# A feed-forward down projection by seven products instead of eight, with its weight sums kept in DRAM

## The chip, the cores and the metric

The kernel runs on one core of one Trainium2 chip. The metric is the device time of one execution in microseconds (us). Before the change it is 3280.02 us, the median of three runs (3275.47, 3280.02 and 3282.64). The engines are TensorE (PE in the profile; PEld is its loading of weights), VectorE (DVE), ScalarE (ACT), GpSimd (POOL) and SyncE (SP). In this kernel SP issues every data transfer. SBUF is the on-chip memory of 128 partitions, PSUM the eight banks into which TensorE writes, DRAM the memory off the core.

## The reference

One layer of a streaming encoder is computed for 2048 prompt frames and 32 sample frames, 2080 columns of 1024 features in all. The layer is token mixing, then attention to 256 memory tokens, then a SwiGLU feed-forward sub-layer; each is wrapped in RMSNorm before and after, and added to the residual. The change touches only the feed-forward part:

```python
def swiglu(h, w_gate, w_up, w_down):
    return (jax.nn.silu(h @ w_gate) * (h @ w_up)) @ w_down

xp = xp + rmsnorm(swiglu(rmsnorm(xp, g_pre_ffn), w_ffn_gate, w_ffn_up, w_ffn_down), g_post_ffn)
```

`w_gate` and `w_up` are 1024 x 2816, `w_down` is 2816 x 1024, all float32.

## The kernel before, in words

**Precision.** A float32 operand is split into a high part (a ScalarE cast) and a low part (a subtraction, on VectorE for weights and for the input, on POOL for the gated activations); this is `split` (lines 424 and 425). `mm3` (line 485) makes a product of three matmuls: high by high, high by low, low by high.

**Blocks and groups.** In the feed-forward stage (line 1710 on) the columns are cut into three blocks `CF` of two halves each, 2 x 348, 2 x 346 and 2 x 346 columns; `ci` numbers the half. The hidden width of 2816 is 22 tiles of 128 rows, and two tiles make a group, 11 groups in all.

**Gate and up by seven products.** `gate_up(g)` (line 1808) makes one group of hidden rows for both column halves. The weight block (1024 x 256) and the input block (1024 x 2n) are each cut in two by two, and the 2 x 2 product is made from seven products instead of eight, of sums of the quarters (`seven_mov` for the input, once in a block, into seven tiles mf; `seven_sta` for the weights, for each group; `unit`, line 1782, for the products, in the PSUM banks X, Y and Z). A unit is 7 x 12 matmuls, a group two units. SiLU and the product with the up part follow, and POOL and ScalarE split the result into the tiles u.

**Down by eight.** `down` (line 1844) takes one group (in the last block the last two together). For each column half and each of eight output tiles it makes one PSUM tile pdn from the group's two row tiles, six matmuls, and VectorE copies it into the accumulator acc (first group, line 571) or adds it (line 532). With the last group come the squares of the post-norm sum (`square`). The weights (`down_w`) are fetched raw, 512 KB a row tile, and split again in each block.

**Buffers.** A block has two accumulators, taken from a pool of two (`xp`), so a new block's accumulator waits for the release of an old one. Raw weights have four buffers of 512 KB (`WRB`), split weights eight (`WSB`), u three, the raw input four (`stage`). The products have six PSUM banks.

**Ends of blocks.** `finish` (line 1872) of a block normalises each half, adds the residual fetched from DRAM and stores it; it is issued after the next block's first and second gate-and-up group. In the last block, half 1 is finished by `finish` and half 0 transposed by `finish_rows`.

**Order.** `Order` (from line 48) writes the order of every engine's instructions and of SP's transfers: it plays the whole program through with a cost for each instruction and the buffer counts, some passes forward and back, and fixes the best order that it found. Each queue then runs strictly in that order.

Of the kernel before, what the change touches and what calls it, by code (L numbers as in the profile page):

```python
# [18 lines left out]
P = 128  # L19
D = 1024  # L20
# [373 lines left out]
def encoder_step(ctx, tc, ins, outs):  # L394
# [118 lines left out]
    qmd = [dpool.tile([D, n], F32, name=f"qmd{b}") for b, (_, n) in enumerate(CB)]  # L513
    biasd = dpool.tile([HA, 768], F32, name="biasd")
# [1196 lines left out]
    UB, WRB, WSB, SGB = 3, 4, 8, 5  # L1711
    with ExitStack() as ph:
# [21 lines left out]
        def ffn_raw(b):  # L1734

            s, n = CF[b]
            raw = {}
            for kh, c in ((0, 0), (0, 1), (1, 1), (1, 0)):
                r = stage(f"hr{b}_{kh}{c}")
                for bb, lo, hi, off in pieces(CB, s + c * n, s + c * n + n):  # L1740
                    SP.dma_start(r[:, :, off : off + hi - lo], h2d[bb][kh * 512 : kh * 512 + 512, lo:hi].rearrange("(k p) n -> p k n", p=P))
                raw[kh, c] = r[:, :, :n]
            return raw

        def ffn_ops(b, raw):

            n = CF[b][1]
            ops = []

            def put(src, eng):  # L1750
                m_ = mps[len(ops)].tile([P, 2, HK, 348], F32R, tag="mov", name=f"mf{b}_{len(ops)}")
                split(m_[:, 0, :, :n], m_[:, 1, :, :n], src, eng)
                ops.append((m_[:, 0, :, :n], m_[:, 1, :, :n]))

            seven_mov(raw, put)
            return ops
# [19 lines left out]
        def prod(ps, w, m, first, last):  # L1776
            mm3(ps, [((w[0][:, k], w[1][:, k]), (m[0][:, k], m[1][:, k])) for k in range(HK)], first, last, not first)
# [23 lines left out]
        QS = ((0, 1), (1, 1), (0, 0), (1, 0))  # L1801
        with tc.high_priority(offset=PRI):
            ops = ffn_ops(0, ffn_raw(0))
        late = []
        for b, (s, n) in enumerate(CF):
            ssqs, silu = {}, []
            acc = [xp.tile([P, KT, 348], F32, tag="acc", name=f"acc{b}_{ci}") for ci in range(2)]
            def gate_up(g, own=False):
                sg = {q: small(sp, "sg", f"sg{b}_{g}_{q[0]}{q[1]}", SGB)[:, :n] for q in QS}
# [218 lines left out]
```

## Time and profile before

| what | value |
|---|---|
| median of three runs | 3280.02 us |
| profiled execution, first to last instruction (its own time is known only by this span) | 3277.0 us |
| TensorE busy | 3156.6 us (96%) |
| VectorE busy | 2416.9 us (74%) |
| ScalarE / POOL busy | 1719.9 / 717.1 us |
| mean granted TensorE clock | 0.984 |
| matmuls of the down projection (tile pdn) | 3168, from 1884.5 to 3261.9 us |
| mean DMA rate | 148 GB/s |

A row of the profile's groups gives line, engine, operation, the tile written and the tiles read, shapes and count, then busy time and mean length, then the idle time of the engine just before these instructions and what ended it. Matmuls are pipelined, so their recorded lengths overlap. A row of waits reads: engine, tile and line, what it waited for, us in total, times, longest.

### The profile page before, as it was taken

The numbers are of one execution on the slowest core, as the hardware profiler recorded it, in microseconds if no ns is written. First come the engines' busy times: TensorE is split into PE (matmuls) and PEld (weight loads), VectorE is DVE, ScalarE is ACT, GpSimd is POOL, SyncE is SP. The second block draws the span as 40 slices with busy tenths as digits, with TensorE's granted clock in tenths as the row PEclk, the third lists the DMA queues.
The fourth block names the chain that finished last, engine by engine and source line by source line (L and its number), as shares of the span: only waits on it lengthen the run. The fifth ranks groups of instructions, "written<-read, shape, count | busy, mean of one in ns | idle before, by whom it ended". The sixth has DMA issues, their size and how long they took to land.

```text
span 3277.0 us, 57899 instructions
## 1 busy us (share of the span) xinstructions
PE 3156.6 (96%) x21387; PEld 3022.0 (92%) x21387; DVE 2416.9 (74%) x4474; ACT 1719.9 (52%) x3706; POOL 717.1 (22%) x933
## 2 busy tenths in 40 slices
PE   7898999799999999999999899999899999899998
PEld 7888999698888888999999799999899999899998
DVE  7976976576575756777777877777977778977776
ACT  5645655656676666566665643334544334444344
POOL 0200100345474545410101111111211111311111
PEclk9999999899999999999999999999999999999999
DMA  5569273876585757765655522222432222422223
GB/s 150 178 168 297 101 222 120 262 227 193 177 269 152 239 169 229 221 191 179 204 175 179 166 91 71 76 78 78 136 111 78 76 73 63 130 79 77 78 78 96
DMA packets 490076, 486.31 MB, mean 148 GB/s; under 512 B 78528, under 2 KB 427881, under 8 KB 489793
## 3 DMA queue, kind: packets, MB, share of 16 engines
q1 hardware_dynamic: 489793, 482.61, 47.2%
q8 instruction: 168, 2.75, 0.3%
q14 instruction: 115, 0.94, 0.1%
HBM read 369.78 MB, written 113.83 MB: 148 GB/s over the span
## 4 chain that ended last, share of the span: by engine, by line
PE 88%; DVE 5%; DMA 3%; ACT 2%; issue 1%; SPq 1%; POOL 0%; DVEq 0%; ACTq 0%; POOLq 0%
PE pdn L485 15%; PE pg_X L485 8%; PE pu_X L485 7%; PE wops L1329 6%; PE mops L485 5%; PE mqps L485 4%; PE pg_Y L485 4%; PE pu_Y L485 4%; PE po L1063 4%; PE s L1058 2%; PE pg_Z L485 2%; PE pu_Z L485 2%; PE pt L1083 2%; PE ms L485 2%; PE g_s L1263 2%; PE wva_X L485 1%
## 5 line engine op out<-in xcount | busy, mean ns | idle before, releaser
L485 PE MATMUL pdn<-u,wd 128*128 128x346 f32 (+1 forms) x3168 | 520.2, 323 | 25.7 <-DVE acc L571 24.4
L485 PEld LDWEIGHTS pdn<-u,wd 128*128 128x128 f32 x3168 | 509.4, 190 | 27.7 <-DVE acc L571 25.3
L425 POOL TENSOR_TENSOR u<-sg,u 128x346 fp32r<-128x346 f32 (+1 forms) x132 | 165.4, 1264 | 1152.9 <-ACT u L424 611.7
L424 ACT CAST wg_s<-wg_r 128x512 fp32r<-128x512 f32 x231 | 139.1, 620 | 480.5 <-PE pdn L485 183.5
L532 DVE TENSOR_TENSOR acc<-acc,pdn 128x346 f32<-128x346 f32 (+1 forms) x464 | 235.8, 513 | 89.1 <-PE pdn L485 88.8
L485 PE MATMUL pg_X<-mf,wg_s 128*128 128x346 f32 (+1 forms) x1584 | 278.1, 324 | 6.6 <-ACT wg_s L424 5.3
L485 PE MATMUL pu_X<-mf,wu_s 128*128 128x346 f32 (+1 forms) x1584 | 275.2, 322 | 0.0
L485 PEld LDWEIGHTS pg_X<-mf,wg_s 128*128 128x128 f32 x1584 | 258.4, 190 | 8.2 <-ACT wg_s L424 5.7
L485 PEld LDWEIGHTS pu_X<-mf,wu_s 128*128 128x128 f32 x1584 | 256.9, 189 | 0.4
L1329 PE MATMUL wops<-om,wo_s 128*128 128x512 f32 (+1 forms) x960 | 214.4, 362 | 0.5 <-POOL om L430 0.5
L485 PE MATMUL mops<-mo,wmo_s 128*128 128x416 f32 x960 | 193.7, 353 | 2.1 <-DVE y L1671 1.2
L425 DVE TENSOR_TENSOR wu_s<-wu_r,wu_s 128x512 fp32r<-128x512 f32 x231 | 155.0, 696 | 39.1 <-ACT wu_s L424 39.0
L425 DVE TENSOR_TENSOR wd<-wd_r,wd 128x512 fp32r<-128x512 f32 x132 | 93.8, 715 | 121.7 <-ACT wd L424 121.6
L485 PEld LDWEIGHTS mops<-mo,wmo_s 128*128 128x128 f32 x960 | 177.1, 188 | 6.7 <-issue 1.9
L1329 PEld LDWEIGHTS wops<-om,wo_s 128*128 128x128 f32 x960 | 149.3, 188 | 20.5 <-issue 2.2
L485 PE MATMUL mqps<-m,wmq_s 128*128 128x416 f32 x768 | 163.6, 357 | 4.7 <-DVE m L430 4.2
L424 ACT CAST wu_s<-wu_r 128x512 fp32r<-128x512 f32 x231 | 136.6, 619 | 50.0 <-DVE wu_r L529 23.2
L425 DVE TENSOR_TENSOR wg_s<-wg_r,wg_s 128x512 fp32r<-128x512 f32 x231 | 158.7, 694 | 0.9 <-ACT wg_s L424 0.7
L1063 PE MATMUL po<-prt,v 128*128 128x128 f32 x1120 | 158.1, 281 | 1.2 <-PE mkps L1329 0.9
L1063 PEld LDWEIGHTS po<-prt,v 128*128 128x128 f32 x1120 | 145.3, 194 | 9.3 <-issue 2.9
L485 PE MATMUL pu_Y<-mf,wu_s 128*128 128x346 f32 (+1 forms) x792 | 140.1, 324 | 7.4 <-DVE up L532 5.7
L485 PEld LDWEIGHTS mqps<-m,wmq_s 128*128 128x128 f32 x768 | 139.8, 189 | 6.8 <-DVE m L430 4.4
(450 smaller groups left out, 7197.0 us busy)
## 6 DMA issues: line engine op xcount, KB each, us to landing
wg_r<-in_w_ffn_gate_dram SPq DMA_DIRECT2D x66, 512.0 KB, 4.4
wu_r<-in_w_ffn_up_dram SPq DMA_DIRECT2D x66, 512.0 KB, 3.5
wd_r<-in_w_ffn_down_dram SPq DMA_DIRECT2D x66, 512.0 KB, 3.4
wmq_r<-in_w_mq_dram SPq DMA_DIRECT2D x80, 256.0 KB, 3.0
wmo_r<-in_w_mo_dram SPq DMA_DIRECT2D x80, 256.0 KB, 3.0
q<-qd SPq DMA_DIRECT2D x32, 512.0 KB, 4.5
wo_r<-in_w_o_dram SPq DMA_DIRECT2D x64, 256.0 KB, 4.1
nb<-nbd SPq DMA_DIRECT2D x16, 640.0 KB, 7.6
```

What stands on the lines that cost most here:

```text
L424: ACT.copy(hi, src)
L425: (lo_eng or DVE).tensor_tensor(out=lo, in0=src, in1=hi.bitcast(F32), op=ALU.subtract)
L485: PE.matmul(ps, lhsT=a, rhs=b, start=first and i == 0, stop=last and i == len(seq) - 1, skip_group_check=skip)
L532: eng.tensor_tensor(out=out, in0=a, in1=b, op=ALU.add)
L1058: PE.matmul(ps_out, lhsT=q[:, 2 * i + e, q0 : q0 + nq], rhs=ks[:, e, k0 : k0 + ncol], start=i == 0, stop=i == 1)
L1063: PE.matmul(po[:, e * P : e * P + n], lhsT=v[:kk, j, e * 64 : e * 64 + P], rhs=prt[:kk, j, :n], start=j == 0, stop=j == len(rows) - 1)
L1083: PE.transpose(ptp[:kk, j, :n], pr[:n, c0 : c0 + kk], ident[:n, :n])
L1263: PE.matmul(sps[bk, li, :], lhsT=lh, rhs=rh, start=True, stop=True)
L1329: PE.matmul(ps, lhsT=a, rhs=b, start=i == 0, stop=i == len(seq) - 1)
```

## The change

Groups 0 to 9 of a block form five pairs. For a pair, the down weights (512 rows of hidden x 1024) and the gated activations (512 rows x 2n columns) are each cut in two by two, and the pair's contribution is made from seven products of sums of quarters. A product has four PSUM tiles, each of two row tiles (six matmuls). Products 0, 2, 4 and 6 go one after the other into the same four banks X; after each of them VectorE adds the banks, as they then stand, to one quarter of the accumulators. Products 1 and 3 do the same in Y, and product 5 in Z. Group 10 keeps the old way, alone, in all three blocks.

The weight sums are made in block 0, split, used, and stored split in DRAM (`wdd`); blocks 1 and 2 fetch the split tiles from there. The activations of three groups are now kept unsplit (`gt`), summed in place and split by POOL and ScalarE in pieces of 2n columns. The two accumulators last through all blocks. The input's staging tiles have half the size (two of four feature tiles, so every block's input is fetched and split in two halves), the residual is fetched and the result stored in quarters instead of halves, and the normalisation factor stays in PSUM.

The diff, cut to its core:

```diff
+    wdd = [dpool.tile([14 * P, 1024], F32, name=f"wdd{j}") for j in range(NF // 4)]
...
-    UB, WRB, WSB, SGB = 3, 4, 8, 5
+    UB, WRB, WSB, GTB = 3, 4, 8, 3
...
+        gt = pool("cgt", GTB)
...
-        pt = ph.enter_context(tc.tile_pool(name="cpt", bufs=1, space=PSUM, **RW))
-        pn = ph.enter_context(tc.tile_pool(name="cpn", bufs=1, space=PSUM, **RW))
+        pn = ph.enter_context(tc.tile_pool(name="cpn", bufs=2, space=PSUM, **RW))
+        accs = [xp.tile([P, KT, 348], F32, tag="acc", name=f"acc{ci}") for ci in range(2)]
         def stage(name):
-            return gp.tile([P, HK, 348], F32, tag="stage", name=name)
+            return gp.tile([P, 2, 348], F32, tag="stage", name=name)
...
+            def u_split(src, name):
+                t = uu.tile([P, 2, 2, 348], F32R, tag="u", name=name)[:, :, :, :n]
+                split(t[:, 0], t[:, 1], src, POOL)
+                return t
...
+            XYZ = (0, 2, 4, 6, 1, 3, 5)
+            def down_sums(j):
+                w = {}
+                with tc.high_priority(offset=PRI):
+                    if b:
+                        for i in XYZ:
+                            w[i] = [wsp(f"wd{b}_{j}_{i}{a}") for a in range(2)]
+                            for a in range(2):
+                                SP.dma_start(w[i][a].bitcast(F32).rearrange("p e m -> p (e m)"), wdd[j][(2 * i + a) * P : (2 * i + a + 1) * P, :])
+                        return w
+                    fs = [[down_raw(4 * j + 2 * k + a) for k in range(2)] for a in range(2)]
+                    def put(i, k, h):
+                        w[i] = [wsp(f"wd{b}_{j}_{i}{a}") for a in range(2)]
+                        for a in range(2):
+                            split(w[i][a][:, 0], w[i][a][:, 1], fs[a][k][:, h])
+                            SP.dma_start(wdd[j][(2 * i + a) * P : (2 * i + a + 1) * P, :], w[i][a].bitcast(F32).rearrange("p e m -> p (e m)"))
+                    def each(f, k, h, x, y):
+                        for a in range(2):
+                            f(DVE, fs[a][k][:, h], fs[a][x[0]][:, x[1]], fs[a][y[0]][:, y[1]])
+                    put(0, 0, 0)
+                    each(sub, 0, 0, (0, 0), (0, 1))
+                    each(add, 0, 1, (0, 1), (1, 1))
+                    put(1, 0, 1)
+                    each(sub, 0, 1, (1, 1), (0, 0))
+                    put(2, 0, 1)
+                    put(4, 0, 0)
+                    put(6, 1, 1)
+                    each(sub, 0, 1, (1, 0), (0, 1))
+                    put(3, 0, 1)
+                    put(5, 1, 0)
+                return w
...
+            def down_seven(j, us):
+                w = down_sums(j)
+                u0, u1 = us
+                b11, b12, b21, b22 = u0[:, :, 0], u0[:, :, 1], u1[:, :, 0], u1[:, :, 1]
+                m = {0: u_split(b11, f"u{b}_{j}_0")}
+                sub(DVE, b12, b22, b12)
+                add(DVE, b11, b11, b12)
+                m[2] = u_split(b11, f"u{b}_{j}_2")
...
+                def prods(i, ps, first):
+                    for q in range(HK):
+                        c = slice(q * P, q * P + P)
+                        mm3(ps[q], [((w[i][a][:, 0, c], w[i][a][:, 1, c]), (m[i][:, 0, a], m[i][:, 1, a])) for a in range(2)], first, True, not first)
+                X = [bank(f"pdX{b}_{j}_{q}") for q in range(HK)]
+                for i, ci, hf in ((0, 0, 0), (2, 1, 0), (4, 1, 1), (6, 0, 1)):
+                    prods(i, X, i == 0)
+                    for q in range(HK):
+                        put_acc(ci, hf * HK + q, X[q], j == 0)
...
-                r = rstd_of(np_, psn[:, :n], n, D, f"n5_{b}_{ci}_r", 2, "nsq", 348)
+                ACT.activation(r, r, AF.Ln, bias=eps_t, scale=1.0 / D)
+                ACT.activation(r, r, AF.Exp, scale=-0.5)
...
+            for g in range(NG):
+                held.append(gate_up(g))
                 if late:
                     late.pop(0)()
+                if not last and g == NG - 2:
+                    raw = ffn_raw(b + 1, 0)
+                if not last and g == NG - 1:
+                    ops = []
+                    ffn_ops(b + 1, 0, raw, ops)
+                    ffn_ops(b + 1, 1, ffn_raw(b + 1, 1), ops)
+                if g and g % 2 == 0:
+                    down_seven(g // 2 - 1, held[g - 2 : g])
```

More of the change, by code (lines that the diff above doesn't have):

```diff
@@ L1842, in square, with put_acc, bank @@
                     add(DVE, ssqs[ci], ssqs[ci], sq)
-            def down(gs, us, cis=(1, 0), dn=None):
-                dn = dn or [down_w(2 * g + j) for g in gs for j in range(2)]
-                us = [ut for u in us for ut in u]
+            def put_acc(ci, m, ps, first):
+                a = acc[ci][:, m, :n]
+                if first:
+                    out(DVE.tensor_copy, a, ps)
+                else:
+                    out(add, DVE, a, a, ps)
+            def bank(name):
+                return pd.tile([P, 512], F32, tag="dense", name=name)[:, :n]
@@ L1855, in down @@
-                        if gs[-1] == NF // 2 - 1:
-                            square(ci, m)
-                            if last and ci == 0:
-                                ACT.mul(acc[ci][:, m, :n], acc[ci][:, m, :n], gains["g_post_ffn"][:, m : m + 1])
+                        ps = bank(f"pdn{b}_{g}_{m}_{ci}")
+                        mm3(ps, [(dn[a][m], (us[ci][:, 0, a], us[ci][:, 1, a])) for a in range(2)])
+                        put_acc(ci, m, ps, False)
+                        square(ci, m)
@@ L1859, in down @@
+                        if last and ci == 0:
+                            ACT.mul(acc[ci][:, m, :n], acc[ci][:, m, :n], gains["g_post_ffn"][:, m : m + 1])
                 return dn
```

131 lines of the change are left out of this document (68 added, 63 removed).

## The prediction

> **What bounds the kernel now.** I read the page first (shares, then the chain), then a table by stretches of the feed-forward stage, then TensorE's waits there, then the groups of instructions by shape.
>
> ```profile
> span 3277.0 us, 57899 instructions
> PE 3156.6 (96%) x21387; PEld 3022.0 (92%) x21387; DVE 2416.9 (74%) x4474; ACT 1719.9 (52%) x3706; POOL 717.1 (22%) x933
> PE 88%; DVE 5%; DMA 3%; ACT 2%; issue 1%; SPq 1%; POOL 0%; DVEq 0%; ACTq 0%; POOLq 0%
> L485 PE MATMUL pdn<-u,wd 128*128 128x346 f32 (+1 forms) x3168 | 520.2, 323 | 25.7 <-DVE acc L571 24.4
> ```
>
> The chain that ends last is TensorE for 88%, and the down projection (pdn) is one of its largest pieces: 3168 matmuls. The mean of 323 ns is of overlapping records, so the price of a matmul comes from stretches where TensorE never stops. Below are eight whole groups of block 0 and of block 1, and then the two stretches in which one block gives way to the next.
>
> ```profile
> 1908.40:2245.60 337.20, 337.20 (x2117) 337.20 (x2116) 245.51 (x422) 133.98 (x260) 43.26 (x33) 1.00 0.24 77
> 2403.20:2738.90 335.70, 335.70 (x2112) 335.70 (x2111) 246.30 (x421) 133.74 (x260) 42.59 (x32) 1.00 0.24 78
> 2300.00:2400.00 100.00, 86.62 (x528) 85.34 (x527) 90.16 (x138) 50.48 (x94) 26.14 (x24) 0.95 0.48 149
> 2800.00:2900.00 100.00, 88.21 (x533) 87.24 (x532) 86.71 (x139) 49.53 (x93) 27.99 (x26) 0.93 0.33 108
> ```
>
> The columns are stretch, length, then busy time and count of PE, PEld, DVE, ACT and POOL, then clock, DMA share and GB/s. In the first two rows TensorE is busy for every microsecond: 337.20/2117 = 159.3 ns a matmul of 348 columns, 335.70/2112 = 159.0 ns of 346. VectorE does 245.51/4 = 61.4 us in each 84.3 us (two groups), 73%. The last two rows lose time: 528 and 533 matmuls of 159 ns are 84.0 and 84.7 us of 100. So a block change costs 16.0 and 15.3 us. The waits say why:
>
> ```profile
> PE pdn L485 <- DVE acc L571: 24.4, 3, 11.9
> PE pu_Y L485 <- DVE up L532: 5.7, 1, 5.7
> PE pg_X L485 <- ACT wg_s L424: 5.3, 1, 5.3
> PE pg_X L485 <- ACT pg_c L571: 0.2, 1, 0.2
> ```
>
> The first down product of a block is copied into an accumulator that the last block is still normalising and storing; TensorE stands, and the clock column shows that it runs slower after.
>
> **The change part by part.**
>
> *Fewer products.* In each block ten of the eleven groups form five pairs. A pair took 2 groups x 2 row tiles x 8 output tiles x 2 column halves x 3 = 192 matmuls and takes 7 x 4 x 2 x 3 = 168. That is 24 x 5 x 3 = 360 fewer, which is also the difference of the two programs' instruction lists; the stages ahead are the same but for a little order late in the memory attention. 120 x 159.3 + 240 x 159.0 ns = **-57.3 us**, all on the engine that sets the end.
>
> *Accumulators.* They were taken anew by each block and first written one group into it. Now they last, and the first write comes behind three groups of gate and up (3 x 168 x 159 ns = 80 us after the change of block) and waits only for the rows that it overwrites. The old block's normalisation is issued inside those 80 us. I take away the whole loss of both stretches, **-31.3 us**; at worst one store stays late (0), at best all of it goes.
>
> *VectorE, block 0.* Rows for the prices; one run of four splits gives the issue time:
>
> ```profile
> 1846.64 2.49 DVE L425 TENSOR_TENSOR wu_s<-wu_r,wu_s 128x512 fp32r<-128x512 f32 x4
> L425 DVE TENSOR_TENSOR wd<-wd_r,wd 128x512 fp32r<-128x512 f32 x132 | 93.8, 715 | 121.7 <-ACT wd L424 121.6
> L532 DVE TENSOR_TENSOR acc<-acc,pdn 128x346 f32<-128x346 f32 x304 | 154.7, 513 | 60.3 <-PE pdn L485 60.2
> L425 DVE TENSOR_TENSOR mf<-hr,mf 128x1384 fp32r<-128x1384 f32 x14 | 22.3, 1596 | 1.1 <-ACT mf L424 1.1
> ```
>
> Four splits in 2.49 us are 0.60 us each, some 0.09 less than their recorded length, since records overlap. By the same step an add from PSUM issues every 0.43, and half of the 1384-wide split takes about 0.79. A pair adds 6 splits of weights (14 for 8), 8 weight sums and 4 sums of the gated activations, and loses 4 adds from PSUM (28 for 32): 14 x 0.60 + 4 x 0.79 - 4 x 0.43 = +9.8 us. VectorE goes from 61.4 of 84.3 to 71.2 of 168 x 3 x 159 ns = 80.2 us, 89%. It still fits beneath TensorE, but two places are bare. (1) The eighth and later weight tiles wait for one of eight buffers: the tile pair of product 3 takes the buffers of product 1, which runs right ahead of it, so a ScalarE cast stands open. (2) All four raw buffers hold the pair's rows until the last splits, so the next gate weights are fetched late; the product that they must beat is 3.8 us away.
>
> ```profile
> L424 ACT CAST wd<-wd_r 128x512 fp32r<-128x512 f32 x132 | 81.4, 621 | 6.2 <-ACT wd L424 3.0 <-ACT sg L1813 1.0 <-PE pg_X L485 0.8
> wg_r<-in_w_ffn_gate_dram SPq DMA_DIRECT2D x66, 512.0 KB, 4.4
> wd_r<-in_w_ffn_down_dram SPq DMA_DIRECT2D x66, 512.0 KB, 3.4
> ```
>
> (1) costs a cast, 0.62, and a handover, some 1 us; (2) a 4.4 us landing and a cast against 3.8 us and a little, so 0 to 4. I take 3 us a pair, **+15** (0 to 40, the upper end from the rivals below). The 14 stores of a pair go through SP's queue, and the next group's four raw loads stand among them, the first behind the tenth tile's store, the last behind the fourteenth's; each of those tiles is split by the time that the load's raw buffer is free, so the queue adds nothing more.
>
> *VectorE, blocks 1 and 2.* No splits or sums of weights there: -8 x 0.60 + 3.2 - 1.7 = -3.3 us a pair; 58 of 80 us. This was hidden time and I price it at nothing. ScalarE (133.98/4 = 33.5 us a pair) and POOL (10.8) gain some 5 and 7 us in block 0 and stay far below.
>
> *Tiles from DRAM.* A pair loads 14 x 512 KB = 7.3 MB where it loaded 2.1. SP holds each load until its buffer is free, and the next group's raw weights stand behind the fourteenth, whose buffer is free once three of seven products are done: 15 us ahead of need, against the 4.4 us above. The queue carries more than this; the DMA view from 1760 to 1890 us, in 40 slices:
>
> ```profile
> GB/s 5 143 51 329 341 365 372 371 321 131 236 220 334 292 208 5 232 292 0 214 4 211 249 357 160 5 2 208 244 131 138 260 201 95 125 6 164 305 220 140
> ```
>
> At 365 GB/s 524 KB pass in 1.4 us; a product uses one in 12 x 159 ns = 1.9 us. I put **+3** in all for ten pairs.
>
> *Input in halves.* The staging tiles shrink to half, so the second half of a block's input is fetched only when the first has been summed. At the first change of block, 37 VectorE instructions stand behind the last down add until the last half is split: 17 half-wide of 0.79, 17 weight operations of 0.60 and 3 adds, 25 us, with some 6 us of matmuls left after it, against 26.7 us of gate and up. So 5 us, and about 3 for the slower clock, as in the stretches above. At the second change the list has the last half split ahead of the last down adds: 2. **+10** (0 to 31, today's loss). At the start of the stage the second halves are fetched behind stores of the last attention block: **+3** (-5 to +8, about the 5.3 and 5.7 waits above).
>
> *The end.*
>
> ```profile
> 3248.53 13.66 PE L485 MATMUL pdn<-u,wd 128*128 128x346 f32 x83
> 3255.01 2.73 DVE L1883 SCALAR_TENSOR_TENSOR acc<-acc,g_post_ffn,n_r 128x346 f32<-128x346 f32 x4
> 3260.96 0.48 ACT L1841 ACTIVATE sq<-acc 128x346 f32<-128x346 f32 x1
> 3261.47 0.59 ACT L1858 ACTIVATE acc<-acc,g_post_ffn 128x346 f32<-128x346 f32 x1
> 3268.20 3.03 DVE L1923 SCALAR_TENSOR_TENSOR xtl<-ytl,rl,xtl 128x512 f32<-128x512 f32 x4 [0.70 <-PE ytl L1919]
> ```
>
> The last two groups shared one down pass; its second half (13.66 us of matmuls) covered the normalisation of the first half. Now that pass has one group, 7.6 us, and the changed list puts the normalisation behind it: 8 scalings of 0.68, 4 adds and two ScalarE passes of 0.5, some 8 us, come ahead of the closing scalings; ScalarE's 8 x (0.48 + 0.59) = 8.6 us also outlast 7.6. **+9** (4 to 12).
>
> *Sum*: 3277.0 - 57.3 - 31.3 + 15 + 3 + 10 + 3 + 9 = 3228.4 for the span. The profiled execution's own time is known only by its span, which is 3.0 below the median of the runs, 3280.02; with the same 3.0 around it I forecast **3231 us**.
>
> **A rule that speaks against it.** POOL's splits get twice as wide.
>
> ```profile
> L425 DVE TENSOR_TENSOR wd<-wd_r,wd x132: 678/693/1457, 1883.9 to 3230.2; 128x512 fp32r<-128x512 f32 x132
> L425 POOL TENSOR_TENSOR u<-sg,u x132: 923/1335/1487, 1884.5 to 3231.1; 128x346 fp32r<-128x346 f32 x88, 128x348 fp32r<-128x348 f32 x44
> ```
>
> The same split of 128x512 takes from 678 to 1457 ns and the same POOL operation from 923 to 1487: each is at times held by the other. A POOL operation of double width (35 a pair in block 0's five pairs, 7 each) lasts some 1.8 to 2.5 us. If each held VectorE for its whole length less a little, 7 x 1.3 = 9 us come on top of 71.2, and VectorE, at 80, is the bound of block 0; with some loss at each handover I put 5 us more on a pair than the 3 above. That is five pairs x 5 us, and it is a rival below. The Trainium skill states it as a rule (SBUF — State Buffer, section "Who interferes with whom"): a VectorE instruction with two SBUF inputs contends with a GpSimd one that reads SBUF, and whoever comes second waits for the whole instruction. The trace agrees in that 1457 is about 678 plus a POOL operation; medians of 693 say that it is rare so far.
>
> **The rivals.** (a) *VectorE becomes the bound of block 0*, as just told: +25 beyond the forecast's +15, about **3256**. For it: 89% before any holding. Against it: the 2300 row has 90.16 us of VectorE in 100, and the wait there was for the accumulator, not for a split.
>
> (b) *Slower: the handover of an accumulating bank.* Each product is added out of PSUM before the next goes into the same four banks; TensorE returns to a bank after 18 matmuls, 2.9 us. In a pair six products wait so. If an add comes late by t, the cost is 15 x 6 x t = 90 t; from t = 0.55 us it eats the whole gain, at 1 us it gives 3231 + 90 = **3321**. For it: VectorE's queue is in order and the adds stand among splits and sums. Against: gate and up do the same at 12 matmuls, 1.9 us, and the wait row shows 0.2 us in all for it.
>
> (c) *Slower: loads do not overlap.* At one 3.4 us landing after another 14 loads take 48 us and have 13 + 25; 9.5 us x 10 pairs give **3326**. The GB/s row speaks against it.
>
> **How the numbers follow.** Forecast 0.60, range of its own 3200 to 3250 (its bounds do not fall together); (a) 0.20; (b) 0.10; (c) 0.04; the rest, small stalls that together eat about the gain, 0.06: 0.02 faster, 0.03 within 0.2% (6.6 us, about what a measurement of this kernel can tell from no change), 0.01 slower. Faster 0.60 + 0.20 + 0.02 = 0.82, same 0.03, slower 0.10 + 0.04 + 0.01 = 0.15. The range 3195 to 3276 holds the forecast's terms and (a) and leaves out (b) and (c).
>
> **What would show it.** Right: 360 fewer matmuls, no TensorE wait for the accumulator copies, VectorE near 90% in block 0 and 75% after, pair periods of 83 and 80 us. Wrong: TensorE waiting for adds from pdX or pdY (b), for weight splits over 3 us a pair (a), or for DMA landings in blocks 1 and 2 (c), or a half clock in the granted-clock slices of block 0, where short stalls would be paid twice.

## The result, and the profile after

The changed kernel takes 3239.64 us (median of four runs, 3234.99 to 3241.13) where the kernel before took 3279.58 beside it: a ratio of 0.9876, 95% interval 0.9862 to 0.9890. The forecast was 3231. The profiled run took 3241.13 us, 1.8 more than its span.

The lines of the page that answer those of before: the span, the engines, the chain that ended last, and the new loads.

```profile
span 3239.3 us, 57597 instructions
PE 3110.5 (96%) x21027; PEld 2969.1 (92%) x21027; DVE 2448.5 (76%) x4513; ACT 1709.8 (53%) x3656; POOL 751.6 (23%) x912
PE 86%; DVE 5%; DMA 3%; issue 2%; ACT 2%; SPq 1%; POOL 1%; DVEq 0%; POOLq 0%; ACTq 0%
wd<-wdd SPq DMA_DIRECT2D x140, 512.0 KB, 4.8
```

There are 360 matmuls fewer, and TensorE still carries the chain. Where the time went is seen in stretches of the feed-forward stage that both kernels share: each block's opening (its first three groups and the down products among them), six further groups, and its end (the last two groups). The columns are those of the prediction's table. First the kernel before, then the changed kernel, each with block 0's opening, its six groups, its end, the opening of block 1, the end of block 1 and the opening of block 2.

```profile
1820.80:1950.60 129.80, 119.83 (x700) 115.84 (x701) 108.54 (x178) 64.65 (x116) 17.54 (x15) 0.95 0.40 127
1950.60:2203.10 252.50, 252.50 (x1587) 252.50 (x1586) 182.87 (x312) 99.95 (x193) 32.45 (x24) 1.00 0.24 76
2203.10:2302.50 99.40, 99.40 (x626) 99.40 (x626) 78.47 (x126) 43.63 (x77) 12.23 (x10) 1.00 0.22 70
2302.50:2430.20 127.70, 114.32 (x702) 113.04 (x702) 111.82 (x176) 61.72 (x116) 28.33 (x26) 0.96 0.44 137
2682.20:2781.40 99.20, 99.20 (x626) 99.20 (x625) 78.70 (x128) 43.90 (x78) 12.60 (x10) 1.00 0.22 71
2781.40:2908.40 127.00, 115.21 (x702) 114.24 (x701) 110.27 (x174) 61.22 (x116) 28.89 (x26) 0.95 0.36 116
```

```profile
1822.60:1956.50 133.90, 117.09 (x677) 113.03 (x677) 122.16 (x192) 67.80 (x119) 21.39 (x13) 0.90 0.53 168
1956.50:2200.10 243.60, 242.68 (x1515) 240.73 (x1514) 213.23 (x353) 110.23 (x206) 38.12 (x21) 1.00 0.47 162
2200.10:2302.70 102.60, 99.17 (x601) 97.02 (x600) 90.43 (x150) 46.83 (x85) 16.65 (x9) 0.98 0.48 168
2302.70:2430.40 127.70, 115.09 (x678) 112.41 (x677) 110.83 (x179) 62.28 (x112) 32.64 (x24) 0.93 0.54 175
2430.40:2671.50 241.10, 241.10 (x1514) 241.10 (x1513) 174.56 (x289) 89.43 (x165) 36.79 (x21) 1.00 0.44 145
2671.50:2768.30 96.80, 95.96 (x603) 95.68 (x602) 86.20 (x137) 44.76 (x78) 14.92 (x8) 1.00 0.48 153
2768.30:2879.20 110.90, 108.97 (x678) 107.67 (x678) 95.27 (x162) 56.68 (x102) 33.00 (x24) 1.00 0.51 169
```

The loss of a stretch is its length less its matmuls at 159.2 ns: 127.70 - 678 x 0.1592 = 19.8 us in the opening of block 1. The first change of block (end of block 0 and opening of block 1) lost -0.3 + 15.9 = 15.6 us before and loses 6.9 + 19.8 = 26.7 now, 11.1 more. The second lost 14.7 and loses 0.8 + 3.0 = 3.8, 10.9 less. The two cancel. The same loss for every kernel that was run, in us, with its time ("before" and "after" mean the two kernels, and what follows the comma is the edit made to it):

| kernel | opening 0 | six groups of 0 | end of 0 | opening 1 | end of 1 | opening 2 | time | ratio to before |
|---|---|---|---|---|---|---|---|---|
| before | 18.4 | -0.2 | -0.3 | 15.9 | -0.5 | 15.2 | 3279.6 | |
| after | 26.1 | 2.4 | 6.9 | 19.8 | 0.8 | 3.0 | 3239.6 | 0.9876 |
| before, lasting accumulators | 18.4 | -0.2 | -0.3 | 12.1 | -0.3 | 13.2 | 3276.7 | 0.9980 |
| before, halves | 19.3 | 0.1 | -0.3 | 13.8 | -0.5 | 14.2 | 3275.8 | 0.9982 |
| before, both | 19.3 | 0.1 | -0.3 | 10.9 | -0.5 | 9.3 | 3269.7 | 0.9966 |
| after, sums in each block | 26.3 | 2.2 | 6.5 | 24.9 | 5.7 | 24.7 | 3283.9 | 1.0010 |
| after, light last pair | 26.0 | 2.0 | 1.7 | 12.0 | 1.0 | 3.0 | 3224.3 | 0.9825 |
| after, additions on VectorE | 25.8 | 2.9 | 6.7 | 20.2 | 1.0 | 7.6 | 3244.0 | 0.9888 |
| after, normalisation first | 25.8 | 2.0 | 7.0 | 12.1 | 1.0 | 3.4 | 3232.0 | 0.9855 |
| after, copies on ScalarE | 21.1 | 1.1 | 6.8 | 17.5 | 0.8 | 2.4 | 3230.0 | 0.9843 |
| after, low parts on VectorE | 23.9 | 1.7 | 14.4 | 5.2 | -0.3 | 3.7 | 3228.8 | 0.9841 |
| after, product moved at the end | 25.8 | 1.8 | 7.0 | 18.3 | 1.0 | 2.9 | 3237.4 | 0.9868 |
| after, three edits | 20.6 | 1.1 | 6.2 | 11.0 | 0.8 | 3.1 | 3226.7 | 0.9836 |
| after, four edits | 20.8 | 0.3 | 11.7 | 5.3 | 0.9 | 3.1 | 3220.5 | 0.9815 |

How far do these figures repeat? The kernel with the product moved at the end has the changed kernel's order of instructions in the feed-forward stage up to 3189 us, so its row is the same work once more: the opening of block 1 differs by 1.5 us, the six groups by 0.6, the other stretches by 0.3 or less. Differences of that size are not told from the spread of a stretch.

TensorE's waits of the changed kernel from 2240 to 2440 us, around the first change (what it waited for, us in total, times, longest):

```profile
PE pdX L485 <- issue: 7.3, 1, 7.3
PE pg_Z L485 <- ACT wg_s L424: 3.9, 1, 3.9
```

The 7.3 us have no releaser by the profile. VectorE's rows at their end show it, in order of time (start, us, operation):

```profile
2396.63 1.54 DVE L1980 SCALAR_TENSOR_TENSOR acc<-acc,g_post_ffn,n_ps 128x348 f32<-128x348 f32 x3
...
2402.13 1.98 DVE L1823 TENSOR_TENSOR g<-g,up 128x346 f32<-128x346 f32 x1
2404.03 0.93 DVE L572 COPY acc<-pdX 128x346 f32<-128x346 f32 x2
```

TensorE goes on at 2404.64, just behind the first copy out of PSUM into the accumulator (2404.03). That copy stood in VectorE's queue behind the old block's normalisation (the scalings of L1980) and behind sums and products of gate and up, one of which took 1.98 us. The stretch of the stall and the one behind it:

```profile
2397.00:2405.00 8.00, 0.72 (x4) 0.47 (x3) 7.91 (x12) 0.77 (x1) 8.00 (x7) 0.72 1.05 395
2405.00:2411.00 6.00, 6.00 (x23) 6.00 (x23) 3.13 (x5) 0.00 (x0) 0.77 (x1) 0.52 1.05 378
```

During the stall VectorE is busy for 7.91 of 8.00 us, and GpSimd for all of them. And the stall is paid again in clock: right behind it the granted clock is 0.52 and a matmul takes 6.00/23 = 0.26 us, 23 x 0.1 = 2.3 us more.

The 3.9 us wait is for the cast of a gate weight of block 1's first group. VectorE was behind there too: ScalarE had cast the first of these weights at 2285.33 us, as soon as it had landed, and VectorE took up its low part at 2296.64, 11 us later, behind splits of the next block's input and additions of pdn.

```profile
2285.33 0.62 ACT L424 CAST wg_s<-wg_r 128x512 fp32r<-128x512 f32 x1 [0.21 <-DMA wg_r<-in_w_ffn_gate_dram]
2296.64 0.69 DVE L425 TENSOR_TENSOR wg_s<-wg_r,wg_s 128x512 fp32r<-128x512 f32 x1
```

### The profile page after: what moved, and what is told of

Its sections match the earlier page's. It is cut to its first block, busy times and chain, and to the rows that moved or that the text cites. A ratio compares the mean times of both kernels' runs of the same rounds, so it can differ in the third digit from the quotient of the medians.

```text
span 3239.3 us, 57597 instructions
## 1 busy us (share of the span) xinstructions
PE 3110.5 (96%) x21027; PEld 2969.1 (92%) x21027; DVE 2448.5 (76%) x4513; ACT 1709.8 (53%) x3656; POOL 751.6 (23%) x912
## 4 chain that ended last, share of the span: by engine, by line
PE 86%; DVE 5%; DMA 3%; issue 2%; ACT 2%; SPq 1%; POOL 1%; DVEq 0%; POOLq 0%; ACTq 0%
PE pg_X L485 7%; PE pu_X L485 7%; PE pdX L485 7%; PE wops L1330 6%; PE mops L485 6%; PE mqps L485 4%; PE po L1064 4%; PE pg_Y L485 4%; PE pu_Y L485 4%; PE pdY L485 3%; PE s L1059 2%; PE pt L1084 2%; PE pg_Z L485 2%; PE pu_Z L485 2%; PE g_s L1264 2%
## 5 line engine op out<-in xcount | busy, mean ns | idle before, releaser
L425 POOL TENSOR_TENSOR u<-g,u 128x692 fp32r<-128x692 f32 (+1 forms) x111 | 199.0, 1799 | 1043.3 <-ACT u L424 862.6
L485 PE MATMUL pdX<-u,wd 128*128 128x346 f32 (+1 forms) x1440 | 241.2, 326 | 10.3 <-issue 7.3
L485 PEld LDWEIGHTS pdX<-u,wd 128*128 128x128 f32 x1440 | 234.8, 192 | 12.6 <-issue 8.3
L424 ACT CAST u<-g 128x692 fp32r<-128x692 f32 (+1 forms) x111 | 84.2, 773 | 231.2 <-PE pdX L485 171.7
L425 DVE TENSOR_TENSOR wu_s<-wu_r,wu_s 128x512 fp32r<-128x512 f32 x231 | 166.9, 746 | 27.3 <-ACT wu_s L424 27.1
L485 PE MATMUL pg_Y<-mf,wg_s 128*128 128x346 f32 (+1 forms) x792 | 141.1, 326 | 1.7 <-ACT wg_s L424 1.4
L533 DVE TENSOR_TENSOR acc<-acc,pdX 128x346 f32<-128x346 f32 (+1 forms) x192 | 96.4, 513 | 59.1 <-PE pdX L485 58.6
```

Source lines behind the costliest of these rows:

```text
L424: ACT.copy(hi, src)
L425: (lo_eng or DVE).tensor_tensor(out=lo, in0=src, in1=hi.bitcast(F32), op=ALU.subtract)
L485: PE.matmul(ps, lhsT=a, rhs=b, start=first and i == 0, stop=last and i == len(seq) - 1, skip_group_check=skip)
L533: eng.tensor_tensor(out=out, in0=a, in1=b, op=ALU.add)
```

## The experiments

**The accumulators and the halves, each alone and together, on the kernel before.**

```diff
+        accs = [xp.tile([P, KT, 348], F32, tag="acc", name=f"acc{ci}") for ci in range(2)]
...
-            acc = [xp.tile([P, KT, 348], F32, tag="acc", name=f"acc{b}_{ci}") for ci in range(2)]
+            acc = accs
```

> The kernel before, with one edit: the two accumulators are allocated once, ahead of the loop over blocks, instead of anew in each block. The prediction's step (the losses of 16.0 and 15.3 us at the two block changes are the wait for accumulators taken anew) as it stands gives about -31 us, 3279.6 to 3248. Theory now: in this kernel the second half's normalisation is issued right ahead of the first down product of a block, so lasting accumulators alone let the copy pass only as far as rows are free, and the first wait moves to a later row; of the 11.9 us wait I expect 3 to 10 us back at each change, 3260 to 3274 in all. Rival: nothing at all (3279), because the normalisation itself is what is late.

```diff
-            return gp.tile([P, HK, 348], F32, tag="stage", name=name)
+            return gp.tile([P, 2, 348], F32, tag="stage", name=name)
...
-                    if g == NF // 2 - 3:
-                        raw = ffn_raw(b + 1)
-                    if g == NF // 2 - 1:
-                        ops = ffn_ops(b + 1, raw)
+                    if g == NF // 2 - 2:
+                        raw = ffn_raw(b + 1, 0)
+                    if g == NF // 2 - 1:
+                        ops = []
+                        ffn_ops(b + 1, 0, raw, ops)
+                        ffn_ops(b + 1, 1, ffn_raw(b + 1, 1), ops)
```

> The kernel before, with one edit: staging tiles of half the size, the input of a block fetched, summed and split in two halves, and the normalisation's residual in quarters. The prediction charged +3 at the start of the stage and +10 at the two block changes: 3293. Theory now: the halves cost this or more at the first change, since VectorE gets the second half's splits only when the first half is summed and the next weights stand behind them: 3290 to 3300. Rival: they cost nothing, the losses at the changes are those of the accumulators: 3280 +- 3.

> The kernel before, with both edits: lasting accumulators and halves, but every down product as before and no weight sums. It stands for the prediction's terms -31.3 + 10 + 3 = -18, so 3261. What the changed kernel's trace shows for the same three places (about -2, -11 and +2) would be about 3268. If it comes out at 3275 or above, the late first write (behind three groups instead of two) is what brings the gain of the second change, not the lasting accumulators.

Measured: 3276.7 (ratio 0.9980, 0.9971 to 0.9990), 3275.8 (0.9982, 0.9973 to 0.9991) and 3269.7 (0.9966, 0.9954 to 0.9977). The opening of block 1 with lasting accumulators, and two of TensorE's waits there, the longest and the one for the accumulator's copy:

```profile
2304.50:2428.40 123.90, 115.77 (x702) 114.63 (x702) 110.47 (x176) 61.20 (x116) 28.51 (x26) 0.96 0.45 142
```

```profile
PE pdn L485 <- DVE sg L1819: 6.8, 1, 6.8
PE pdn L485 <- DVE acc L571: 1.4, 1, 1.4
```

They save 3.8 us there and 2.0 in the opening of block 2, less than the 6 to 20 that I expected and a fifth of the prediction's 31.3: the 11.9 us wait for the copy becomes 1.4, and 6.8 come up in its stead, for a product of gate and up (L1819) that stands in VectorE's queue. The halves were to cost 13 or more; the openings of blocks 1 and 2 lose 2.1 and 1.0 us *less* with them, and the opening of block 0 0.9 more. So my theory of the halves fell, and 3275.8 lies a little under the rival's 3277 to 3283 as well. Together they save 5.0 and 5.9, and 3269.7 is nearest to the 3268 that was read off the changed kernel's trace. I read the wait at a block change as a full VectorE queue in which the accumulator's copy came last; the 6.8 us that came up say so. These runs keep the first write one group into the block. What the late first write alone would do on this kernel was not run.

**The weight sums in each block, on the changed kernel.** The branch that loads them is never taken, and the stores are made in block 0 alone.

```diff
-                    if b:
+                    if False:
                         for i in XYZ:
...
+                            if not b:
```

> The changed kernel, with one edit: blocks 1 and 2 compute and split the sums of the down weights again instead of loading them from DRAM (block 0 still stores them). The prediction priced the relief of VectorE in blocks 1 and 2 at nothing, and block 0's loaded VectorE at 3 us a pair; measured in block 0 are 1.0 us in a regular pair and 5.7 in the first one. Theory now: blocks 1 and 2 then look like block 0 (10 us each), and the second block change like the first (some 15 us more than now): 3240 to 3265 +- 8. Rival: only the pair price, +10 to +20, with the change of block as it is: 3250 to 3260. Second rival: VectorE at 89% is fully hidden, 3240 +- 4, and the DRAM copies are worth nothing.

Measured: 3283.9, ratio 1.0010 (1.0000 to 1.0021): the whole gain is gone. Three pairs of block 1, its end, and the opening of block 2:

```profile
2439.80:2682.20 242.40, 242.31 (x1513) 240.38 (x1512) 218.02 (x351) 110.97 (x207) 38.80 (x21) 1.00 0.24 77
2682.20:2783.60 101.40, 98.12 (x601) 96.72 (x601) 94.21 (x153) 48.13 (x89) 16.41 (x9) 0.98 0.25 78
2783.60:2916.40 132.80, 118.32 (x679) 115.16 (x678) 116.09 (x192) 67.18 (x121) 29.58 (x23) 0.92 0.38 117
```

A regular pair hardly cares: 242.4/3 = 80.8 us with VectorE busy for 218.02/242.40 = 90%, against 241.1/3 = 80.4 at 72%. The second change cares: 5.7 + 24.7 = 30.4 us lost against 3.8. TensorE's two longest waits there are for VectorE:

```profile
PE pu_X L485 <- DVE up L533: 5.3, 1, 5.3
PE pdX L485 <- DVE acc L572: 2.9, 1, 2.9
```

What DRAM buys is this 26.6 us and 5.1 at the opening of block 1. The rest of the difference of the two spans is 5 us ahead of the stage (its first matmul is at 1827.4 instead of 1822.6; the planner orders the early stages otherwise in this kernel, from 177 us on, so this part is not the edit's own work) and some us in the last pairs and the end. All three of my cases were too low: the theory ended at 3273, with 15 us more at the second change and 10 in a block; it had the place right and the size too small.

**Is it the last loaded pair of block 0?** This run leaves out the fifth pair's own weight sums: in every block that pair takes those of the fourth from DRAM. VectorE then forms and splits none for it in block 0.

```diff
-                    if b:
+                    if b or j == 4:
...
-                                SP.dma_start(w[i][a].bitcast(F32).rearrange("p e m -> p (e m)"), wdd[j][(2 * i + a) * P : (2 * i + a + 1) * P, :])
+                                SP.dma_start(w[i][a].bitcast(F32).rearrange("p e m -> p (e m)"), wdd[min(j, 3)][(2 * i + a) * P : (2 * i + a + 1) * P, :])
```

> The changed kernel, with one edit that makes its output wrong: the fifth pair of every block takes the weight sums of the fourth pair, loaded from DRAM, so in block 0 VectorE forms and splits no sums in the last pair ahead of the first change of block (14 splits and 8 sums fewer). Everything else is the same work. Theory (the first change is dear because VectorE comes to it with a backlog from the last loaded pair of block 0): the end of block 0 falls from 7.2 us of loss to 1 to 2, the opening of block 1 from 20.7 to 4 to 8, as at the second change; 3239.6 to 3218 to 3224. Rival (the opening's price is the normalisation held by the GpSimd additions, or the input in halves, whatever came before): only the 5 us at the end of block 0 go, 3235, and the 7 us wait of the first pair of block 1 stays.

Measured: 3224.3, ratio 0.9825 (0.9808 to 0.9841). End of block 0 and opening of block 1:

```profile
2196.50:2294.20 97.70, 97.04 (x603) 95.72 (x602) 87.90 (x142) 45.81 (x82) 16.71 (x9) 1.00 0.50 171
2294.20:2414.10 119.90, 112.31 (x678) 110.40 (x677) 101.30 (x163) 56.10 (x102) 31.93 (x24) 0.97 0.53 171
```

26.7 us fall to 1.7 + 12.0 = 13.7. Half of the loss at the first change is thus the price of one loaded pair, and most of that half (7.8 us) shows only behind the change, in block 1. The run does not single out VectorE's 14 splits and 8 sums: ScalarE's 14 casts and SP's 14 stores go with them, and the raw buffers come free, so that the gate weights of block 1's first group are requested at 2243 and 2245 us instead of 2277 and 2280. That it is the backlog of VectorE rests on the rows of the stall and of the gate weight above. The opening stays dearer than I expected (12.0, not 4 to 8).

**Who holds VectorE in the opening?** Three edits, each alone: the residual additions on VectorE, the normalisation with priority, the first copies on ScalarE.

```diff
-                        add(DVE if last and k % 2 else POOL, a[:, k, :n], a[:, k, :n], xr[:, k - k2, :n])
+                        add(DVE if k % 2 or not last else POOL, a[:, k, :n], a[:, k, :n], xr[:, k - k2, :n])
```

> The changed kernel, with one edit: the 32 residual additions of the normalisations after blocks 0 and 1 run on VectorE and not on GpSimd (about 0.5 us each, 16 us more VectorE work). Theory (backlog): VectorE has more to do at the first change, so +3 to +8 there (3243 to 3248), nothing at the second. Rival (GpSimd holds VectorE: products of gate and up took 1.9 us there and 0.5 elsewhere): the holding goes and the 7.3 us wait with it, -5 to -10, 3230 to 3235.

```diff
-                    late.pop(0)()
+                    with tc.high_priority(offset=PRI):
+                        late.pop(0)()
```

> The changed kernel, with one edit in the order alone: the normalisation of the last block has priority, so that its second half starts 77 matmuls (some 12 us) earlier. Theory (backlog): the same work is only in another order; the 7.3 us wait for the first copy shrinks or goes (-3 to -10 at the first pair of block 1), and part of it comes back as waits for splits of the gate and up weights (+0 to +5): 3231 to 3240. Rival (late normalisation alone is the cause): the whole 10 us of that pair go and nothing comes back, 3229.

```diff
-                    out(DVE.tensor_copy, a, ps)
+                    out(ACT.copy, a, ps)
```

> The changed kernel, with one edit: the sixteen first copies into the accumulators (first pair of each block) run on ScalarE and not on VectorE (16 x some 0.5 us, 8 us of VectorE work in that pair). Theory (backlog): the copies no longer stand behind the normalisation in VectorE's queue; the 7.3 us wait goes for the most part and half a clock's worth with it, -5 to -9 at the first change, -1 to -3 in the first pair of block 0: 3228 to 3234. Rival: the copy waits for the rows to be stored and not for VectorE, so it stays, 3238 to 3241.

Measured: 3244.0 (0.9888, 0.9873 to 0.9903), 3232.0 (0.9855, 0.9840 to 0.9871) and 3230.0 (0.9843, 0.9829 to 0.9858). The first two intervals overlap that of the changed kernel, so there the stretches have to tell. With the additions on VectorE the first change stays where it was (26.9 us) and the second loses 4.8 more; 3244.0 lies in the range of my theory, but by luck: I had 3 to 8 us more at the first change and nothing at the second. The rival missed too. The first copy's wait is 4.2 us there instead of 7.3 and the loss is the same, so I take it that VectorE spent what GpSimd gave back; the run does not show it apart. The normalisation first takes 7.7 us off the opening of block 1, the size of the 7.3 us wait. From the priority's run and from the copies' run, the opening of block 1, and from the latter block 0's opening and ScalarE's first copies:

```profile
2298.90:2419.10 120.20, 113.34 (x679) 109.70 (x678) 108.00 (x178) 63.20 (x112) 31.31 (x24) 0.97 0.60 185
```

```profile
1820.30:1949.00 128.70, 114.73 (x676) 111.66 (x677) 111.52 (x175) 73.59 (x134) 20.90 (x13) 0.91 0.53 172
2293.70:2419.10 125.40, 114.60 (x678) 111.60 (x677) 102.31 (x163) 69.70 (x128) 32.43 (x24) 0.95 0.54 178
```

```profile
2393.76 0.80 ACT L572 COPY acc<-pdX 128x346 f32<-128x346 f32 x2 [2.70 <-DMA out_dram<-acc]
```

The time of the copies' run is what I expected, its place is not: 5.0 us come from the first opening, where no old block is in the way, and 2.3 from block 1, little more than the spread. There the copy, out of VectorE's queue, waits for the store of the row that it overwrites. So the wait for the accumulator is there again (TensorE's longest between 2240 and 2440 us), now for the store that ends the old block's normalisation:

```profile
PE pdX L485 <- ACT acc L572: 5.4, 1, 5.4
```

**GpSimd's share: the low parts on VectorE.**

```diff
-                split(t[:, 0], t[:, 1], src, POOL)
+                split(t[:, 0], t[:, 1], src, DVE)
```

> The changed kernel, with one edit: the low parts of the gated activations (111 of some 1.8 us on GpSimd) are formed on VectorE (some 0.8 us each; 7 a pair, +5.5 us, so 76.7 of 80.2 us in block 0 and 63.7 after). Theory (holding by GpSimd is small, VectorE's load is what counts): regular pairs of block 0 lose 2 to 4 us instead of 0.9, each opening 3 to 8 us more: 3250 to 3265. Rival (a) of the prediction (GpSimd's wide operations hold VectorE for their length): VectorE is relieved by more than it is charged, 3225 to 3237.

Measured: 3228.8, ratio 0.9841 (0.9824 to 0.9857). My theory missed and rival (a)'s side was right. The same stretch of block 0, first the changed kernel, then this one; then VectorE's groups in it in the same order:

```profile
1956.50:2200.00 243.50, 242.58 (x1514) 240.63 (x1513) 213.13 (x352) 110.23 (x206) 38.12 (x21) 1.00 0.47 162
```

```profile
1956.50:2200.00 243.50, 242.74 (x1517) 241.79 (x1517) 219.47 (x377) 112.94 (x210) 0.00 (x0) 1.00 0.48 169
```

```profile
L425 DVE TENSOR_TENSOR wd<-wd_r,wd 128x512 fp32r<-128x512 f32 x42 | 34.1, 822 | 0.2
L533 DVE TENSOR_TENSOR acc<-acc,pdX 128x348 f32<-128x348 f32 x48 | 23.2, 509 | 6.4 <-PE pdX L485 6.2
```

```profile
L425 DVE TENSOR_TENSOR wd<-wd_r,wd 128x512 fp32r<-128x512 f32 x42 | 28.3, 685 | 1.3 <-ACT wd L424 1.3
L533 DVE TENSOR_TENSOR acc<-acc,pdX 128x348 f32<-128x348 f32 x48 | 23.9, 512 | 5.4 <-PE pdX L485 5.2
L425 DVE TENSOR_TENSOR u<-g,u 128x696 fp32r<-128x696 f32 x21 | 18.4, 876 | 0.3 <-ACT u L424 0.3
```

VectorE takes on 18.4 us and its busy time rises by 219.47 - 213.13 = 6.3. GpSimd's 21 operations had held it for at least 12.1 us, 0.57 each, which is a third of their own 38.12/21 = 1.82. The splits of the down weights, with two inputs in SBUF, fall from 822 to 685 ns, those of the up weights from 760 to 686; those of the gate weights were not held (684 and 685). The additions from PSUM, with one input in SBUF, do not fall (509 and 512). The Trainium skill (SBUF — State Buffer, section "Who interferes with whom") has both as a rule: VectorE contends with GpSimd's reads when it has two SBUF inputs, and not with one; these rows agree. In the six groups this changes 0.7 us, no more than the spread: VectorE was hidden there. At the first change 26.7 us become 14.4 + 5.2 = 19.6: the opening is nearly free, and a wait of 9.8 us for a low part turns up in block 0's last pair. The edit also takes the low parts out of GpSimd's queue and forms each in 0.88 us instead of 1.82; how much of the gain at the change is this and how much is VectorE's release is not told apart.

**The end.** The last product of `down_seven` with its additions becomes a function, `last_prod`, which the last block calls between the closing steps.

```diff
+                if hold:
+                    return last_prod
+                last_prod()
...
-                    down_seven(g // 2 - 1, held[g - 2 : g])
+                    rest = down_seven(g // 2 - 1, held[g - 2 : g], last and g == NG - 1)
...
                 finish(1, lambda k: xr1[:, k : k + 2])
+                rest()
                 down(NG - 1, held[-1], (0,), dn)
```

> The changed kernel, with one edit: in the last block the fifth pair's last product (24 matmuls, 3.8 us) stands behind the last group's products of the second column half, so that it covers part of that half's normalisation. The end, from the start of the last down matmul, is 22.6 us (15.2 before the change). Theory (the prediction's: the closing normalisation stands ahead of the last scalings on VectorE, and cover was lost): -2 to -4 us, 3236 to 3238. Rival: ScalarE's squares and scalings of the last half set the end whatever stands before them: within 1 us of the changed kernel.

Measured: 3237.4, ratio 0.9868 (0.9853 to 0.9883), not to be told from the changed kernel's. It lies in the range of my theory, but the place that the theory speaks of, the end, hardly moved. From TensorE's last down matmul to the end it takes 22.2 us instead of 22.6. TensorE's rows behind its last down matmuls:

```profile
3212.40 0.75 PE L1978 MATMUL n_ps<-ssq,ones 128*128 128x346 f32 x2
3220.84 1.32 PE L2010 MATMUL nl_ps<-ones,ssq 128*128 128x1 f32 x6 [7.70 <-DVE ssq L533]
```

The matmul of the first half's norm is still behind the last down products in the order, so nothing is covered; TensorE then waits 7.7 us for VectorE's last addition of squares, which stands behind the eight scalings. The rival's outcome, but not its reason.

**Together.** The priority, the copies and the edit of the end; and then a fourth, the low parts on VectorE except in block 0's fifth pair and each block's last group:

```diff
+            def u_split(src, name, eng=POOL):
...
+                split(t[:, 0], t[:, 1], src, eng)
...
+                eng = POOL if b == 0 and j == 4 else DVE
+                m = {0: u_split(b11, f"u{b}_{j}_0", eng)}
```

> The changed kernel with three of the edits together: the normalisation with priority, the first copies on ScalarE, and the last product of the fifth pair behind the last group's first half. If each acts in its own place (the first opening -5 and regular pairs -1 by the copies, the second opening -8 to -11 by priority and copies together, the end -2 to -4), 3218 to 3225. If the copies and the priority cure the same wait, so that only one counts, 3225 to 3230.

> The three edits together and a fourth: the low parts of the gated activations on VectorE, but on GpSimd in the fifth pair of block 0 and in the last group of each block (where the run with all of them on VectorE lost a 9.8 us wait of TensorE for one that stood behind the next block's input splits). If the places add up: the first opening 21.4 to about 19, the end of block 0 about 7 as with GpSimd, the opening of block 1 11.9 to 5 to 8, the rest as with three edits, so some 5 to 9 us under its 3226.7: 3217 to 3222. If the late splits of block 0's last pair are what makes the opening of block 1 dear (and not GpSimd's holding there), the opening stays at 10 to 12 and the time at 3223 to 3227.

Measured: 3226.7 (0.9836, 0.9821 to 0.9851) and 3220.5 (0.9815, 0.9798 to 0.9832). The last is faster than both kernels, by 1.85% and, by the two ratios, 0.6%. The time with three edits falls in my second case, but the places speak for the first: the first opening gains 5.5 us, the six groups 1.3, and the opening of block 1 8.8, where priority and copies alone gained 7.7 and 2.3. So the two cures overlap by 1.2 us at most, no more than the spread. What is missing is the end, 22.0 us instead of 22.6. End of block 0 and opening of block 1 with four, and TensorE's longest wait in them:

```profile
2188.90:2296.60 107.70, 98.39 (x603) 97.16 (x602) 102.22 (x165) 53.23 (x95) 17.91 (x9) 0.95 0.48 163
2296.60:2406.50 109.90, 105.69 (x657) 104.43 (x657) 92.25 (x150) 62.34 (x118) 17.46 (x16) 1.00 0.57 190
```

```profile
PE pdY L485 <- ACT u L424: 9.3, 1, 9.3
```

The opening is at 5.3 us as expected, the end of block 0 at 11.7 instead of 7: one 9.3 us wait for a cast of the fifth pair. ScalarE's row for that cast says what it waited for, a sum of gated activations on VectorE:

```profile
2266.49 2.12 ACT L424 CAST u<-g 128x696 fp32r<-128x696 f32 x3 [0.87 <-DVE g L530]
```

and VectorE's rows what stood ahead of that sum, the next block's input (hr and mf):

```profile
2260.54 1.79 DVE L530 TENSOR_TENSOR hr<-hr,hr 128x692 f32<-128x692 f32 x2
...
2264.74 0.87 DVE L425 TENSOR_TENSOR mf<-hr,mf 128x692 fp32r<-128x692 f32 x1
2265.52 0.88 DVE L530 TENSOR_TENSOR g<-g,g 128x696 f32<-128x696 f32 x1
...
2267.11 7.72 DVE L425 TENSOR_TENSOR mf<-hr,mf 128x692 fp32r<-128x692 f32 x4
```

In this stretch VectorE is busy for 102.22 of 107.70 us, 95%: it has next to no slack there. And the four splits that follow take 7.72 us, 1.9 each where the one before took 0.87, while GpSimd does three of this pair's low parts (6.74 us from 2267.34 on).

## Why the prediction was right or wrong

The sign and the main term were right, and the forecast was too low by 10.9 us on the span (3228.4 against 3239.3). By its own steps:

*Fewer products*: 21387 - 21027 = 360, and the pairs of block 1 run at 80.4 us, 504 matmuls at 159.5 ns. Right.

*Accumulators and input in halves*, -31.3 + 10 = -21.3: measured +11.1 at the first change and -10.9 at the second, +0.2 in all. This is the step that failed, and nearly all of it at the first change, where I had -16.0 + 8 = -8. The sentence that failed is "I take away the whole loss of both stretches". At the first change 26.7 us are lost where the forecast left 8. It took the row with the wait for an accumulator's copy as the cause, where the copy was the last of a full VectorE queue: lasting accumulators alone, without the late first write, save 5.8 us, not 31.3, and the halves alone cost nothing. And it took VectorE's 89% in block 0 as something that "still fits beneath TensorE": true in a steady pair, but the queue came to the change of block with the last pair's work undone. Taking the loaded pair away saves 13.0 us there. What the other half (13.7 us) is made of stays open. The last run's rows show the next block's input splits ahead of the pair's own sums; the order of the normalisation, the first copies moved to ScalarE and the low parts moved to VectorE each take 2 to 8 us of the change away, and what they share is not known. The kernel before with both edits has 10.6 us in the same place.

*Blocks 1 and 2, VectorE's relief, priced at nothing*: right in the pairs (80.8 us without it, 80.4 with), wrong at the second change, where without it 26.6 us are lost. So the second change came out near the forecast (-13.3, measured -10.9) by luck: the reason given is not enough. The kernel with the sums in each block has lasting accumulators and the first write three groups later too, and loses 24.7 us in the same opening. It takes the relief that was priced at nothing; how much of the rest the late write does is not shown.

*Block 0 and the start*, +15 + 3: measured 7.7 in the opening and 2.6 in the six groups, 10.3. VectorE's load was right, 213.23/3 = 71.1 us a pair (71.2 forecast, 88%) and 174.56/3 = 58.2 in block 1 (58). The price was 3 us a pair and is 0.9. The pair periods are 81.2 and 80.4 (83 and 80).

*Tiles from DRAM*, +3: nothing. In the six groups of block 1 TensorE is busy for 241.10 of 241.10 us, though a load takes 4.8 us to land. Rivals (b) and (c) fall with the same row: no stall for an addition out of pdX or pdY, none for a load.

*The end*, +9: 7.5, 22.6 us behind the start of the last down matmul (3239.3 - 3216.7) where it was 15.1 (3277.0 - 3261.9). The reason given fits VectorE's rows: the closing normalisation waits for its factor until 3221.69, behind the last down matmul, and the closing scalings start when it is through.

```profile
3221.69 1.06 DVE L1980 SCALAR_TENSOR_TENSOR acc<-acc,g_post_ffn,n_ps 128x346 f32<-128x346 f32 x2 [2.71 <-ACT n_ps L1975]
3229.13 4.03 DVE L2019 SCALAR_TENSOR_TENSOR xtl<-ytl,rl,xtl 128x512 f32<-128x512 f32 x6
```

*Not in the sum*: the stage starts 1.8 us later (1822.6 against 1820.8). Runs whose instructions up to there are the same as the changed kernel's have 1818.8 to 1820.5, so this is the spread between runs.

Sum: -57.3 + 0.2 + 10.3 + 7.5 + 1.8 = -37.5; the spans differ by 37.7. That it closes so well is in part luck, since a stretch repeats only within 1.5 us.

*Rival (a)* had a mechanism that is real and a place that is not. GpSimd's wide operations hold VectorE, by some 0.57 us each instead of 1.3, and without them the kernel is 10.9 us faster; but the regular pairs of block 0 lose 0.8 us each, and the price falls due at the changes of block. (Two slips of the prediction here, which its sum does not use: the "35 a pair" are 35 in block 0 in all, seven a pair; and 1457 ns is 678 and 779 more, which is less than the shortest GpSimd operation, 923, and so not a whole one.)

## What to carry to other kernels

A share of 89% is a steady figure: price a loaded engine at the place where its stage ends and the next one's extra work begins, by the backlog that it brings there, not by its share. The releaser named at a stall is the last entry of a queue; before taking the whole stall away with it, ask what stands ahead in the queue, since that is what will be late next. And a relief that is worth nothing in the steady loop can be worth most of the gain at the stage's edges: the run without the DRAM copies lost some 31 us more at the two changes of block, of a gain of 40, though its pairs are only 0.4 us longer.

## What the runs showed of the hardware

I had not expected GpSimd's holding to be so plain in one pair of rows: the same 42 splits of 128x512 at 822 and 685 ns with and without GpSimd's 21 operations, beside additions out of PSUM at 509 and 512. Nor had I priced that a 7.3 us stall of TensorE is followed by 6 us at a granted clock of 0.52, some 2.3 us more, a third of the stall. With the normalisation first both are gone (190 matmuls in 30.00 us, granted clock 1.00, from 2389 to 2419 us), but the opening gains 7.7 us and not 9.6, since smaller waits come up elsewhere.
